# A hybrid decoder layer with expert retrieval on one core: gathers spread into the last expert group, one low half in four on GpSimd in the down stage, and one root chain with two output queues at the end

## The chip, the cores and the metric

The kernel runs on one core of one Trainium2 chip. The metric is the device time of one execution in microseconds (us), the median over the runs shown. A core has five instruction streams that matter here: TensorE (PE, matrix products), VectorE (DVE), ScalarE (ACT), GpSimd (POOL) and the sync engine (SP), which only issues transfers (DMAs). Each works through its own queue in order, and semaphores tie the queues together. PE writes to a small accumulator memory (PSUM); everything else lives in the on-chip buffer (SBUF) or in the device's main memory (HBM).

## The reference: what is computed

One decoder layer on 512 tokens of width 2048, in fp32. A first half mixes the tokens (projection, a gated MLP over the sequence, a matrix-memory recurrence, an output projection). The second half, where the change is, is a retrieval layer over 16384 experts: each token scores two sets of 128 keys per head, keeps 8 x 16 experts, and computes

```python
u_sel = peer_u.astype(xc.dtype)[eidx]
v_sel = peer_v.astype(xc.dtype)[eidx]
act = jax.nn.gelu(jnp.einsum("td,thkd->thk", xc, u_sel))
return jnp.einsum("thk,thkd->td", gate * act, v_sel)
```

That is followed by the residual sum and a last RMS norm: `x / sqrt(mean(x*x) + eps) * final_g`.

## The kernel before

**Two ways to the same sum.** For the last 352 tokens (`TD`) the kernel computes every expert, with dense products, and multiplies by a dense matrix of gates `Wd` that is zero where an expert is not chosen. For the first 160 tokens (128 and `G2` = 32 more) it gathers only the chosen rows of `peer_u` and `peer_v` with indirect DMAs, 128 rows (1 MB) in each, and DVE works on them. There are 2 x 128 + 2 x 32 = 320 gathers. Both ways run at the same time: PE does the dense one, and the gathers are spread over it.

**The dense way** has two stages. In the up stage (tile `pu`), for each of 128 groups of experts, the weights `in_u` are multiplied with the tokens. In the down stage (tile `pv`), 16 groups of experts (`g`) times 4 column chunks (`ch`) times 4 pieces (`pc`) of `in_v` are multiplied with `C`, the gated activations, which `product(g)` prepares one group ahead (`At` from `Ad`, `Wt` from `Wd`, lines 741 to 750 and 82). A piece is 128 x 1024 weights and 24 matmuls. To keep fp32 accuracy on a faster matmul type each operand is split in a high half (a rounded copy, ACT, line 109, tile `whi`) and a low half (the difference, line 110, tile `wlo`), and `mm3` issues three matmuls: line 118 and 119 need the high half of the weight, line 120 its low half.

**The path of a piece.** SP issues a 1 MB transfer `raw<-in_v` (line 102) that holds two pieces. There are two `raw` buffers, so SP waits until both low halves of the transfer two before are made. When it has landed, ACT makes two high halves, DVE two low halves, and PE uses them. `queue` holds `LA` = 3 pieces of lookahead. At the end of each chunk DVE adds four PSUM banks into `acc` (tile `top`, line 896: the evictions; one operand in PSUM, one in SBUF).

**The gathers.** `gather_step` is called after each piece and hands out gathers by a budget: the number left over the slots left, weighted with a share. A gather (line 572, on POOL) may not start before PE has finished the piece four calls earlier (`pace`), and needs one of three buffers `g`. DVE then reduces it: for `peer_u` a multiply and sum (line 608; the tokens lie in PSUM as `hps` in the up stage, in SBUF as `h` later), for `peer_v` a multiply and add into `acc0` or `acc1` (line 623, both inputs in SBUF).

**POOL's low halves.** In the up stage all low halves are put off (`defer["on"]`, list `pending`), and each `peer_u` gather's reduction hands one to POOL, with a dependency on a one-element DVE memset, the mark (tile `flag`, line 604). In the down stage before the change DVE makes all of them.

**Order.** The program is written in this order, but a scheduler with its own timeline then places the instructions of each engine. What stands in a queue is therefore read from the built program's order, as shown below.

**The end.** `settle` adds each finished chunk of 512 columns to the residual `xf` (three tiles of tokens, 96, 128 and 128 rows), with squares for the norm. For the last chunk it computes the root per tile and writes two halves per tile, six transfers, all on SP (line 875).

The lines of the budget and of the down loop before the change:

```python
gathers = {"left": 2 * P + 2 * G2, "slots": NP - 2 + NPC + nv - 24 - 28, "owed": 0.0}
...
def gather_step(last, share=1.0):
    pace.append(last.ins)
    gathers["owed"] += share * gathers["left"] / max(gathers["slots"], 1)
    gathers["slots"] -= share
...
for pc in range(GE // 2):
    hi, lo = take()
    if n + LA < nv:
        queue.append(next(weights))
```

## Time and profile before

| what | value |
|---|---|
| median of 3 runs | 2972.83 us (2971.12 to 2982.24) |
| the profiled execution: its time, its span | 2967.64 us, 2965.9 us |
| granted TensorE clock over the span | 0.991 |
| PE busy over the span | 2892.1 us (98%) |
| DVE, ACT, POOL busy | 2163.5, 1132.8, 794.1 us |
| HBM traffic | 798 MB, 269 GB/s over the span |

The up stage runs from about 820 to 1926 us of the span, the down stage from 1926 to about 2948 us. An engine's busy time is the union of its instructions' spans; PE's matmuls overlap, so PE can be busy without being at its peak. A row of a group gives line, engine, operation, tiles written and read, shapes and count; behind the bar total and mean duration, then the idle time in front and what ended it. "SPq" and the like are issuing instructions.

### The profile page before, as it was taken

To read this page: it belongs to the slowest core of one execution; us is meant where nothing else is said; L and a number is where in the kernel's file an instruction comes from. 1 tells how busy PE (TensorE), PEld (TensorE's weight loads), DVE (VectorE), ACT (ScalarE), POOL (GpSimd) and SP (SyncE) were. 2 spreads that over 40 slices of the span, in tenths; PEclk is the share of its full clock that TensorE was granted. 3 is DMA by queue.
4 is the path that set the end of the run, shared out by engine and by line. 5 is a ranking of instruction groups with operands and counts; after the bars stand their busy time and mean duration, and the time that the engine had idled before them with its cause. 6 is when DMAs were issued, how large, how long until landed. Compare 5 with 4: busy or idle time off the path is not lost.

```text
span 2965.9 us, 41624 instructions
## 1 busy us (share of the span) xinstructions
PE 2892.1 (98%) x16709; PEld 2725.1 (92%) x16709; DVE 2163.5 (73%) x3026; ACT 1132.8 (38%) x1635; POOL 794.1 (27%) x494
## 2 busy tenths in 40 slices
PE   9999999999999999999999999999999999999997
PEld 7888888887799999999999999999999999999997
DVE  5534333324696989979888887679988998889955
ACT  5322244323242333333676675323222323232333
POOL 0000000000046666565554211121232322223300
PEclk9999999999999999999999999999999999999999
DMA  6223222325379898888888888889999999999852
GB/s 241 86 86 121 86 92 93 102 97 178 114 272 349 337 344 335 308 336 299 334 341 344 336 346 335 321 322 367 376 358 344 365 364 344 375 341 368 338 199 105
DMA packets 147091, 800.78 MB, mean 270 GB/s; under 512 B 15168, under 2 KB 37744, under 8 KB 68656
## 3 DMA queue, kind: packets, MB, share of 16 engines
q1 hardware_dynamic: 87616, 401.68, 36.8%
q0 software_dynamic: 50064, 373.36, 33.3%
q10 hardware_dynamic: 9216, 23.07, 2.0%
q8 instruction: 131, 2.15, 0.3%
q14 instruction: 64, 0.52, 0.0%
HBM read 741.39 MB, written 56.62 MB: 269 GB/s over the span
## 4 chain that ended last, share of the span: by engine, by line
PE 80%; DVE 10%; DMA 6%; issue 2%; ACT 1%; SPq 0%; POOL 0%; ACTq 0%; DVEq 0%; POOLq 0%
PE pu L120 9%; PE pu L118 9%; PE pu L119 9%; PE pv L120 8%; PE pv L118 8%; PE pv L119 8%; PE pn L118 4%; PE pn L119 4%; PE pn L120 4%; DVE wlo L110 3%; PE pwb L725 3%; PE po L118 2%; PE po L120 2%; PE po L119 2%; DMA raw<-in_v 2%
## 5 line engine op out<-in xcount | busy, mean ns | idle before, releaser
L109 ACT ACTIVATE whi<-raw 128x1024 fp32r<-128x1024 f32 x512 | 526.9, 1055 | 850.6 <-DMA raw<-in_v 391.6
L120 PE MATMUL pu<-Th,wlo 128*128 128x352 f32 x2048 | 666.3, 325 | 17.5 <-DVE wlo L110 13.3
L118 PE MATMUL pu<-Th,whi 128*128 128x352 f32 x2048 | 673.7, 329 | 3.0 <-ACT whi L109 3.0
L118 PE MATMUL pv<-C,whi 128*128 128x352 f32 x2048 | 661.6, 324 | 6.7 <-ACT ast L795 3.9
L119 PE MATMUL pu<-Tl,whi 128*128 128x352 f32 x2048 | 664.4, 324 | 0.0
L119 PE MATMUL pv<-C,whi 128*128 128x352 f32 x2048 | 660.9, 323 | 0.0
L120 PE MATMUL pv<-C,wlo 128*128 128x352 f32 x2048 | 597.2, 325 | 16.1 <-DVE wlo L110 16.1
L110 DVE TENSOR_TENSOR wlo<-raw,whi 128x1024 fp32r<-128x1024 f32 x384 | 480.8, 1269 | 101.8 <-ACT whi L109 101.7
L572 POOL DMA_INDIRECT g<-in_peer_v,eidx x160 | 258.4, 1615 | 732.4 <-PE pv L120 276.6
L82 DVE TENSOR_TENSOR wlo<-raw,whi 128x1024 fp32r<-128x1024 f32 x130 | 159.2, 1225 | 350.4 <-ACT whi L81 350.1
L120 PEld LDWEIGHTS pu<-Th,wlo 128*128 128x128 f32 x2048 | 388.0, 189 | 19.9 <-DVE wlo L110 15.4
L120 PEld LDWEIGHTS pv<-C,wlo 128*128 128x128 f32 x2048 | 376.0, 189 | 22.3 <-DVE wlo L110 21.4
L118 PEld LDWEIGHTS pv<-C,whi 128*128 128x128 f32 x2048 | 386.7, 189 | 8.8 <-ACT ast L795 4.2
L623 DVE SCALAR_TENSOR_TENSOR acc<-g,gate,acc 128x2048 f32<-128x2048 f32 x160 | 375.8, 2348 | 23.5 <-DMA g<-in_peer_v,eidx 22.8
L118 PEld LDWEIGHTS pu<-Th,whi 128*128 128x128 f32 x2048 | 388.2, 190 | 4.5 <-ACT whi L109 4.0
L119 PEld LDWEIGHTS pu<-Tl,whi 128*128 128x128 f32 x2048 | 388.2, 190 | 0.4
L119 PEld LDWEIGHTS pv<-C,whi 128*128 128x128 f32 x2048 | 386.4, 189 | 0.8 <-issue 0.8
L110 POOL TENSOR_TENSOR wlo<-raw,whi 128x1024 fp32r<-128x1024 f32 x128 | 318.8, 2497 | 102.1 <-ACT whi L109 91.3
L608 DVE CUSTOM_DVE_ANT_0 g<-hps,g 128x2048 f32<-128x2048 f32 x128 | 291.6, 2283 | 44.5 <-DMA g<-in_peer_u,eidx 32.9
L572 POOL DMA_INDIRECT g<-in_peer_u,eidx x160 | 195.1, 1220 | 446.4 <-PE pv L120 99.8
L81 ACT ACTIVATE whi<-raw 128x1024 fp32r<-128x1024 f32 x130 | 137.6, 1058 | 443.6 <-PE pn L120 243.1
L119 PE MATMUL pn<-wlo,Th 128*128 128x512 f32 x512 | 205.1, 401 | 0.0
(275 smaller groups left out, 3510.4 us busy)
## 6 DMA issues: line engine op xcount, KB each, us to landing
raw<-in_u SPq DMA_DIRECT2D x128, 1024.0 KB
raw<-in_v SPq DMA_DIRECT2D x128, 1024.0 KB
raw<-in_w_in SPq DMA_DIRECT2D x80, 512.0 KB
Ad<-ast ACTq DMA_DIRECT2D x64, 352.0 KB
Wd<-wst POOLq DMA_DIRECT2D x11, 2048.0 KB
At<-Ad SPq DMA_DIRECT2D x32, 704.0 KB
raw<-in_w_out SPq DMA_DIRECT2D x32, 512.0 KB
Wt<-Wd SPq DMA_DIRECT2D x32, 512.0 KB
```

What stands on the lines that cost most here:

```text
L81: nc.scalar.activation(hi, src, AF.Copy)
L82: nc.vector.tensor_tensor(lo, src, hi.bitcast(F32), op=ALU.subtract)
L109: nc.scalar.activation(hi, part, AF.Copy)
L110: low = [lambda eng, lo=lo, part=part, hi=hi: eng.tensor_tensor(lo, part, hi.bitcast(F32), op=ALU.subtract)]
L118: nc.tensor.matmul(o, sh, mh, start=start, stop=False)
L119: nc.tensor.matmul(o, sh, ml, start=False, stop=False)
L120: return nc.tensor.matmul(o, sl, mh, start=False, stop=stop)
L572: i = nc.gpsimd.indirect_dma_start(out=g, out_offset=None, in_=table, in_offset=bass.IndirectOffsetOnAxis(ap=ix[:, q:q + 1], axis=0))
L608: nc.vector.tensor_tensor_reduce(out=g, in0=late["h"] if n == 0 and "h" in late else h[n], in1=g, op0=ALU.mult, op1=ALU.add, scale=1.0, sc ...
L623: nc.vector.scalar_tensor_tensor(acc[n], g, gt[:, q:q + 1], acc[n], op0=ALU.mult, op1=ALU.add)
L725: nc.tensor.matmul(pw[:, i * P:(i + 1) * P], o2[:, i, :], o1[:, i, :], start=True, stop=True)
```

## The change

The diff:

```diff
@@
                 mybir.DependencyClass.Sync, mybir.DependencyReason.DATA), reason="pace")
         return g
 
+    def beside():
+        while pending and not pending[0]:
+            pending.pop(0)
+        if pending:
+            mark = nc.vector.memset(flag, 0.0)
+            i = pending.pop(0).pop()(nc.gpsimd)
+            tc.add_manual_dep(i.ins, mark.ins.name, mybir.DependencyInfo(
+                mybir.DependencyClass.Sync, mybir.DependencyReason.DATA), reason="beside")
+
     acc2 = []
     late = {}
     DEPTH = 2
@@
                     h[1] = late["pool"].tile([P, D], F32, tag="h21", name="h21")
                     nc.sync.dma_start(h[1], h2d[1])
                 if n == 0 and "h" in late:
-                    while pending and not pending[0]:
-                        pending.pop(0)
-                    if pending:
-                        mark = nc.vector.memset(flag, 0.0)
-                        i = pending.pop(0).pop()(nc.gpsimd)
-                        tc.add_manual_dep(i.ins, mark.ins.name, mybir.DependencyInfo(
-                            mybir.DependencyClass.Sync, mybir.DependencyReason.DATA), reason="beside")
+                    beside()
                 nc.vector.tensor_tensor_reduce(out=g, in0=late["h"] if n == 0 and "h" in late else h[n], in1=g, op0=ALU.mult, op1=ALU.add, scale=1.0,
                                                scalar=0.0, accum_out=act[:, q:q + 1])
                 return
@@
     NPC = 2 * NE
     nv = 2 * NE
     exps = experts()
-    gathers = {"left": 2 * P + 2 * G2, "slots": NP - 2 + NPC + nv - 24 - 28, "owed": 0.0}
+    TURN = 0.6
+    gathers = {"left": 2 * P + 2 * G2, "slots": NP - 2 + NPC - 30 + 30 * TURN + 12 * TURN + nv - 12 - 14, "owed": 0.0}
 
     def gather_step(last, share=1.0):
         pace.append(last.ins)
@@
             if e % 2 == 1:
                 o = e % GE - 1
                 nc.scalar.dma_start(Ad[e // GE][:, o:o + 2, :], ast)
-        gather_step(last, 1.0 if begun is None else 0.45)
+        gather_step(last, 1.0 if begun is None else TURN)
         if not started:
             if not advance(first, 1):
                 started = n + 1
@@
         toks.append((at, min(P - at % P, T - at)))
         at += toks[-1][1]
     sq3 = vp.tile([P, 3, 4], F32, name="sq3")
+    nc.vector.memset(sq3, 1.0)
     ss3 = vp.tile([P, 4], F32, name="ss3")
     r3 = vp.tile([P, 4], F32, name="r3")
 
@@
             nc.scalar.activation(vp.tile([P, 512], F32, name="sj")[0:rows, 0:w.stop - w.start], o, AF.Square,
                                  accum_out=sq3[0:rows, j, ch:ch + 1])
             nc.vector.tensor_tensor(o, o, fg[0:rows, d], op=ALU.mult)
-            if not done:
-                continue
-            nc.vector.tensor_reduce(ss3[0:rows, j:j + 1], sq3[0:rows, j, :], axis=AX.X, op=ALU.add)
-            rstd(r3[0:rows, j:j + 1], ss3[0:rows, j:j + 1], D)
+        if not done:
+            return
+        nc.vector.tensor_reduce(ss3[:, 0:3], sq3, axis=AX.X, op=ALU.add)
+        rstd(r3[:, 0:3], ss3[:, 0:3], D)
+        for j, (t0, rows) in enumerate(toks):
             for hf in range(2):
-                s = slice(hf * 1024, (hf + 1) * 1024)
-                o = xf[j][0:rows, s]
+                o = xf[j][0:rows, hf * 1024:(hf + 1) * 1024]
                 if hf:
                     nc.scalar.activation(o, o, AF.Copy, scale=r3[0:rows, j:j + 1])
                 else:
                     nc.vector.tensor_scalar(o, o, r3[0:rows, j:j + 1], None, op0=ALU.mult)
-                nc.sync.dma_start(out[t0:t0 + rows, s], o)
+                (nc.sync, nc.gpsimd)[hf].dma_start(out[t0:t0 + rows, hf * 1024:(hf + 1) * 1024], o)
+
+    pick = vp.tile([P, G2], F32, name="pick")
+    nc.vector.tensor_reduce(pick, ident.rearrange("p (s t) -> p t s", t=G2), axis=AX.X, op=ALU.add)
+
+    def last_rows():
+        y = acc2[0]
+        for ch in range(4):
+            d = slice(ch * 512, (ch + 1) * 512)
+            ph = bank(("mm", "sm")[ch % 2], f"ph{ch}")
+            nc.tensor.matmul(ph[0:G2, :], pick, y[:, d], start=True, stop=True)
+            nc.scalar.activation(y[0:G2, d], ph[0:G2, :], AF.Copy)
+        finish(G2, y, hg.tile([P, D], F32, tag="g", name="junk", bufs=3), P)
 
     n = 0
     for g in range(NG):
@@
             for pc in range(GE // 2):
                 hi, lo = take()
                 if n + LA < nv:
+                    defer["on"] = pc == GE // 2 - 1
                     queue.append(next(weights))
+                    defer["on"] = False
                 for db in range(4):
                     last = part(pc, db, hi, lo)
                 n += 1
-                gather_step(last, 0.45 if n <= 12 else 1.0)
+                gather_step(last, TURN if n <= 12 else 1.0)
                 m = 4 * ch + pc
                 if m >= 10 or m % 2 == 0:
                     advance(nxt, 1)
+            beside()
             for db in range(4):
                 close(db)
             if g == NG - 1:
+                if ch == 1:
+                    assert gathers["left"] == 0, gathers
+                    advance(exps, 1)
+                    last_rows()
                 settle(ch, range(4), False)
         if g == NG - 2:
-            assert gathers["left"] == 0
-            advance(exps, 1)
-            y = acc2[0]
-            pick = vp.tile([P, G2], F32, name="pick")
-            nc.vector.tensor_reduce(pick, ident.rearrange("p (s t) -> p t s", t=G2), axis=AX.X, op=ALU.add)
-            for ch in range(4):
-                d = slice(ch * 512, (ch + 1) * 512)
-                ph = bank(("mm", "sm")[ch % 2], f"ph{ch}")
-                nc.tensor.matmul(ph[0:G2, :], pick, y[:, d], start=True, stop=True)
-                nc.scalar.activation(y[0:G2, d], ph[0:G2, :], AF.Copy)
-            junk = hg.tile([P, D], F32, tag="g", name="junk", bufs=3)
-            finish(G2, y, junk, P)
-            xf += [hg.tile([P, D], F32, tag="g", name=f"xf{j}", bufs=3) for j in range(3)]
+            xf += [At[0].rearrange("p j t -> p (j t)")[:, 0:D], Wt[0].rearrange("p b j t -> p (b j t)")[:, 0:D],
+                   hg.tile([P, D], F32, tag="h20", name="xf2")]
             for j, (t0, rows) in enumerate(toks):
                 nc.sync.dma_start(xf[j][0:rows, :], x2d[t0 // P, t0 % P:t0 % P + rows, :])
 
```

So the gathers' budget has 487.2 slots instead of 460, and the gathers end inside the last group of experts instead of before it; the residual tiles `xf` now lie in buffers that are free earlier, since the `g` buffers are still in use. Of the four pieces fetched during a chunk the last one's low half is put off and handed to POOL where the chunk's evictions are written, with the same kind of mark as in the up stage. At the end one chain of small operations serves all three tiles, and the second half of each tile's output goes out over POOL's queue.

Three places in the built programs' order. The first is DVE's queue before the up stage, while the query weights are split (line 82); `flag` is the mark that POOL's low halves wait for. The last marks of before, and what follows them:

```order
L604 MEMSET flag_4784 1x1 x26
L82 TENSOR_TENSOR wlo_4980<-raw_4978,whi_4979 128x1024
L604 MEMSET flag_4784 1x1 x27
L82 TENSOR_TENSOR wlo_5010<-raw_5008,whi_5009 128x1024
L604 MEMSET flag_4784 1x1 x9
L82 TENSOR_TENSOR wlo_5048<-raw_5046,whi_5047 128x1024
```

The same place after:

```order
L583 MEMSET flag_4784 1x1 x26
L82 TENSOR_TENSOR wlo_4980<-raw_4978,whi_4979 128x1024
L583 MEMSET flag_4784 1x1 x27
L82 TENSOR_TENSOR wlo_5010<-raw_5008,whi_5009 128x1024
L583 MEMSET flag_4784 1x1 x26
L82 TENSOR_TENSOR wlo_5048<-raw_5046,whi_5047 128x1024
L583 MEMSET flag_4784 1x1 x27
L82 TENSOR_TENSOR wlo_5094<-raw_5092,whi_5093 128x1024
L583 MEMSET flag_4784 1x1
L492 MAX val_5076<-sc_5080 128x8 x2
L583 MEMSET flag_4784 1x1
L493 MAX_INDEX ind_5077<-val_5076,sc_5080 128x8 x2
```

All 128 marks before, and all 191 after, are placed there, far ahead of the stages whose low halves wait for them; the 63 new ones have not moved to the evictions.

The second place is POOL's queue in the down stage, at the fourth group of experts. Numbers tell the buffers apart; `wlo_18244` is the low half of a piece, `raw` and `whi` its transfer and its high half. Before:

```order
L572 DMA g_18441<-in_peer_v,eidx_4618 128x2048
L572 DMA g_18475<-in_peer_v,eidx_4618 128x2048
L572 DMA g_18537<-in_peer_v,eidx_4618 128x2048
L572 DMA g_18578<-in_peer_v,eidx_4618 128x2048
L572 DMA g_18642<-in_peer_v,eidx_4618 128x2048
L572 DMA g_18675<-in_peer_v,eidx_4618 128x2048
L572 DMA g_18745<-in_peer_v,eidx_4618 128x2048
L572 DMA g_18776<-in_peer_v,eidx_4618 128x2048
```

After:

```order
L572 DMA g_18373<-in_peer_v,eidx_4618 128x2048
L110 TENSOR_TENSOR wlo_18244<-raw_18241,whi_18243 128x1024
L572 DMA g_18444<-in_peer_v,eidx_4618 128x2048
L572 DMA g_18478<-in_peer_v,eidx_4618 128x2048
L572 DMA g_18539<-in_peer_v,eidx_4618 128x2048
L572 DMA g_18582<-in_peer_v,eidx_4618 128x2048
L110 TENSOR_TENSOR wlo_18380<-raw_18377,whi_18379 128x1024
L572 DMA g_18646<-in_peer_v,eidx_4618 128x2048
L572 DMA g_18678<-in_peer_v,eidx_4618 128x2048
L110 TENSOR_TENSOR wlo_18513<-raw_18510,whi_18512 128x1024
L572 DMA g_18750<-in_peer_v,eidx_4618 128x2048
L572 DMA g_18781<-in_peer_v,eidx_4618 128x2048
```

A low half now stands after every two to four gathers, in one queue with them: it starts when the gathers ahead of it are issued and its high half is made, and the gathers behind it wait for it. In DVE's queue 63 rows of line 110 are gone (384 before, 321 after).

The third place is the end of SP's queue. Before:

```order
L938 DMA xf_24109<-x2d 96x2048
L938 DMA xf_24110<-x2d 128x2048
L938 DMA xf_24111<-x2d 128x2048
L846 DMA out<-acc_22275 32x2048
L102 DMA raw<-in_v 128x2048 x4
L875 DMA out<-xf_24109 96x1024 x2
L875 DMA out<-xf_24110 128x1024 x2
L875 DMA out<-xf_24111 128x1024 x2
L999 UNCONDITIONAL_BRANCH
```

After, the end of SP's queue:

```order
L951 DMA Wt_15254<-x2d 128x2048
L102 DMA raw<-in_v 128x2048 x5
L951 DMA At_15253<-x2d 96x2048
L102 DMA raw<-in_v 128x2048 x13
L851 DMA out<-acc_22766 32x2048
L880 DMA out<-At_15253 96x1024
L880 DMA out<-Wt_15254 128x1024
L880 DMA out<-xf_24133 128x1024
L1012 UNCONDITIONAL_BRANCH
```

After, the end of POOL's:

```order
L110 TENSOR_TENSOR wlo<-raw,whi 128x1024
L572 DMA g<-in_peer_v,eidx_4783 128x2048 x3
L110 TENSOR_TENSOR wlo<-raw,whi 128x1024
L572 DMA g<-in_peer_v,eidx_4783 128x2048
L110 TENSOR_TENSOR wlo<-raw,whi 128x1024 x3
L880 DMA out<-At_15253 96x1024
L880 DMA out<-Wt_15254 128x1024
L880 DMA out<-xf_24133 128x1024
L1012 UNCONDITIONAL_BRANCH
```

The six transfers of the output are three and three now; the two loads of `xf` that stood behind the bulk of `raw<-in_v` are 13 and 18 transfers ahead of its end (the third, `xf_24133`, is further ahead still).

## The prediction

> **What bounds the kernel now.** I read the page first, then the granted clock, then the down stage cut into stretches, then the waits of PE, SP and POOL in it, and last the groups of DVE. The page and the stretches (columns: length, then busy time and count of PE, weight loads, DVE, ACT, POOL, then granted clock, DMA share, GB/s):
>
> ```profile
> span 2965.9 us, 41624 instructions
> 1926.00:2080.00 154.00, 153.65 (x951) 153.66 (x952) 126.43 (x109) 44.82 (x43) 33.05 (x24) 0.99 0.91 346
> 2080.00:2780.00 700.00, 681.10 (x4199) 674.87 (x4198) 628.76 (x557) 210.13 (x203) 209.23 (x121) 0.99 0.94 358
> 2780.00:2878.00 98.00, 98.00 (x615) 97.63 (x614) 69.04 (x67) 30.17 (x30) 15.55 (x8) 1.00 0.66 246
> 2878.00:2948.00 70.00, 70.00 (x432) 66.31 (x431) 37.58 (x55) 25.57 (x39) 0.00 (x0) 1.00 0.36 121
> 2948.00:2966.00 18.00, 1.08 (x10) 0.84 (x8) 7.59 (x31) 5.93 (x12) 0.00 (x0) 0.68 0.45 161
> ```
>
> PE is the bound nearly everywhere. It loses time in one place of the down stage, from 2080 to 2780 us: 18.9 us of 700. There DVE is busy for 629 of 700 us (89.8%) and the DMA engines 94%. In the stretch before, at 82% and 91%, PE loses 0.35 us; behind 2780 us, where the gathers thin out and end, it loses nothing. So the place for a gain is 18.9 us of idle PE and what the clock loses after such pauses:
>
> ```profile
> 2200.00:2300.00 100.00, 95.87 (x587) 95.00 (x586) 87.94 (x72) 28.84 (x28) 29.90 (x17) 0.98 0.93 356
> 2400.00:2500.00 100.00, 95.43 (x573) 94.26 (x574) 87.59 (x83) 32.06 (x32) 25.61 (x17) 0.97 0.93 348
> ```
>
> 0.02 and 0.03 of 100 us are 5 us of clock. What PE waits for there, and SP and POOL:
>
> ```profile
> PE pv L120 <- DVE wlo L110: 16.1, 17, 2.6
> ...
> SPq L102 <- DVE wlo L110: 402.9, 80, 10.2
> ...
> SPq L745 <- DVE At L750: 74.8, 10, 12.6
> ...
> POOL g L572 <- PE pv L120: 267.7, 66, 8.4
> ```
>
> PE waits for low halves, 17 times; SP waits to issue the next transfer of weights until the low halves of an older one are made; so a late DVE makes the transfer late, and this the next high and low half. POOL mostly waits for PE's pace, which is harmless. What DVE does in these 700 us:
>
> ```profile
> L110 DVE TENSOR_TENSOR wlo<-raw,whi 128x1024 fp32r<-128x1024 f32 x176 | 209.9, 1219 | 6.9 <-ACT whi L109 6.9
> L623 DVE SCALAR_TENSOR_TENSOR acc<-g,gate,acc 128x2048 f32<-128x2048 f32 x89 | 209.1, 2349 | 9.1 <-DMA g<-in_peer_v,eidx 8.7
> L896 DVE TENSOR_TENSOR top<-pv,top 128x352 f32<-128x352 f32 x175 | 88.0, 520 | 50.5 <-PE pv L120 48.0
> L608 DVE CUSTOM_DVE_ANT_0 g<-h,g 128x2048 f32<-128x2048 f32 x32 | 72.9, 2287 | 0.4 <-DMA g<-in_peer_u,eidx 0.3
> L82 DVE TENSOR_TENSOR C<-At,C 128x1408 fp32r<-128x1408 f32 x22 | 35.7, 1621 | 3.7 <-ACT C L81 3.4
> L750 DVE TENSOR_TENSOR At<-At,Wt 128x1408 f32<-128x1408 f32 x22 | 35.7, 1621 | 0.0
> ```
>
> All but the evictions (L896) have both tensors in SBUF: 209.9 + 209.1 + 72.9 + 35.7 + 35.7 = 563 us, 80% of the time.
>
> **The change, part by part.** The sum is made against the profiled execution, 2967.6 us, and its differences are put on the median, 2972.8, which is 5.2 us (0.17%) above it.
>
> *Gathers spread further.* 320 gathers over 487.2 instead of 460 slots: 5.6% thinner. In the 700 us there are 121 (89 + 32 rows above), so 7 fewer: 7 x 2.35 = 16 us less DVE, and 7 MB less of 358 GB/s x 700 us = 251 MB, 2.8%. Against this stand the loads of `xf`, 2.9 MB in all, of which the first two now fall in or just behind this stretch (1 to 2 MB), and one more wait of the kind SP on L750, 7.5 us each (74.8 by 10), which lies before a transfer and may or may not reach PE. Net some 5 MB, 2%, and the DMA share falls to about 0.92, near the stretch without loss. The load goes to 2780 to 2870 us, where DVE has 29 of 98 us free and the DMA share is 0.66: some 7 x 2.35 = 16 us more DVE, 87% then.
>
> *One low half in four to POOL.* DVE loses 44 of 176: 44 x 1.22 = 54 us. But the order shows the marks in DVE's queue before the up stage, 2000 us ahead, so nothing ties a POOL low half to the evictions; it starts when its turn comes in POOL's queue. What it then does to DVE the up stage shows, where 128 of them run. First the group, then two meetings:
>
> ```profile
> L110 POOL TENSOR_TENSOR wlo<-raw,whi 128x1024 fp32r<-128x1024 f32 x128 | 318.8, 2497 | 102.1 <-ACT whi L109 91.3 <-PE pwb L725 4.1 <-DVE inf L515 1.3
> L110 DVE TENSOR_TENSOR wlo<-raw,whi 128x1024 fp32r<-128x1024 f32 x64 | 96.8, 1514 | 26.3 <-ACT whi L109 26.3
> ...
> 1388.08 2.40 POOL L110 TENSOR_TENSOR wlo<-raw,whi 128x1024 fp32r<-128x1024 f32 x1
> 1387.69 3.88 DVE L110 TENSOR_TENSOR wlo<-raw,whi 128x1024 fp32r<-128x1024 f32 x1
> ...
> 941.10 2.41 POOL L110 TENSOR_TENSOR wlo<-raw,whi 128x1024 fp32r<-128x1024 f32 x1
> 942.21 2.29 DVE L608 CUSTOM_DVE_ANT_0 g<-hps,g 128x2048 f32<-128x2048 f32 x1 [2.54 <-DMA g<-in_peer_u,eidx]
> ```
>
> A DVE subtraction with both inputs in SBUF takes 3.88 instead of 1.22 us beside POOL's 2.40: it stands still while POOL works. A DVE operation with one input in PSUM (`hps`) keeps its 2.29. Over the up stage the 64 DVE low halves take 1.51 instead of 1.22 us. By this row alone POOL's 128 cost DVE 64 x 0.30 = 19 us, 0.15 each: the lower bound. The upper is a whole POOL operation, 2.41. In the down stage 80% of DVE's time are such operations, so a POOL operation at a random moment costs 0.80 x 2.41 = 1.9 us; some will fall beside evictions, and I take 1.6, nearer to the upper end for that share. Then DVE's account is 54 saved, 44 x 1.6 = 70 paid: +16 us, and the thinner gathers give 16 back. DVE's share stays at 90%. Both ends for the range: from 54 + 16 - 7 = 63 us less (81%, as in the stretch without loss) to 54 + 16 - 106 = 36 us more (95%).
>
> The Trainium skill (SBUF — State Buffer, section "Who interferes with whom") says that a VectorE instruction with two SBUF inputs and a GpSimd one that reads SBUF exclude each other for the whole instruction, and that the one that issues first keeps the other waiting. The 3.88 above agrees, and by that rule alone each low half outside the evictions costs the full 2.41; what that gives is the second rival.
>
> *POOL's queue.* A low half waits at its head for its high half, with gathers behind it. In the up stage PE waited for a POOL low half once in 128:
>
> ```profile
> PE pu L120 <- DVE wlo L110: 13.3, 6, 4.2
> PE pu L120 <- POOL wlo L110: 4.1, 1, 4.1
> ...
> L572 POOL DMA_INDIRECT g<-in_peer_v,eidx x89 | 158.8, 1784 | 353.0 <-PE pv L120 167.9 <-DVE acc L623 97.0 <-DVE top L896 30.4
> ```
>
> 63 new ones at that rate are 2 us. The upper bound: where a gather ahead is released late, it takes 1.78 us, then DVE's running operation up to 2.35, then 2.41, 6.5 together against less than two pieces (a piece is 700 us / 175 = 4.0); a fifth of the 63 late by 1 us each are 13 us. I take 3.
>
> *Result for the down stage.* With DVE unchanged and the DMA share halfway back to where nothing is lost, I take a third off: 18.9 / 3 + 5 / 3 = 8 us gained. The rate that is left, 12.6 us in 700, goes on for 90 us: 1.6 lost. POOL late: 3 lost. Net -3.4.
>
> *The up stage.* POOL and DVE do the same work with gathers 5.6% thinner at first and denser at the turn (0.6 for 0.45). Its waits are 17.4 us in the two rows above, and a new order may move them either way by 5; I take -1.
>
> *`last_rows`.* Moved, not new, into a part where PE is 100% and DVE 54% busy (37.58 of 70). Zero, as long as the last gather is reduced before PE comes to it; two chunks are left to hide it.
>
> *The end.* SP's six issues, and the two engines that feed them:
>
> ```profile
> 2954.61 5.55 SPq L875 DMA_DIRECT2D out<-xf  x6
> ...
> 2953.82 3.23 ACT L872 ACTIVATE xf<-xf,r 96x1024 f32<-96x1024 f32 x3 [0.56 <-DVE r L78]
> ...
> 2954.76 1.41 DVE L874 TENSOR_SCALAR xf<-xf,r 128x1024 f32<-128x1024 f32 x2
> ```
>
> The last half tile is ready at 2957.05 (ACT), the last issue ends at 2960.16. With two queues the issue is no longer 3.1 us behind, but 2.9 MB at the 346 to 358 GB/s of the stretches above take 8 us, and the end is at 2965.9, 11.3 us after the first issue. So at most 3 us, at least -1 (a slower start on POOL's queue); I take 1.4 gained. The single root chain makes the first tile wait for the third, and spares small operations: zero. The Trainium skill (DMA: Bandwidth & Descriptors, section "Issuing engines are not separate DMA queues") has transfers of all issuing engines run on the same 16 engines; by that too the second queue can spare issue time alone.
>
> Sum: -3.4 - 1 - 1.4 = -5.8, rounded to -6: **2967 us**, 0.2% under the median and within the 0.5% (15 us) that a measurement of this kernel can tell from no change.
>
> **The rivals.** *Faster:* POOL's low halves fall beside evictions or idle time after all ((88 + 71) / 700 = 23% of DVE's time are evictions or idle), DVE drops to 81%, the DMA share to 0.92, and the down stage runs like 1926 to 2080 us. Then 18.9 + 5 go, the up stage gives some 2, the end 1.4: -27, 2946 us. For it: PE waits for nothing but low halves. Against it: the marks tie nothing, and 80% of DVE's time is of the kind that stands still. From half of this on, -15, it counts as faster. *Slower:* each POOL low half holds DVE for its full length: DVE 95%. From 82% to 90% PE's loss went from 0.2% to 2.7%, 0.32% per point; 5 points more are 1.6% of 800 us at the least, 13 us, and twice that if it goes on steepening, plus up to 13 for late POOL halves: +15 to +39, say 2995 us. It decides from a cost per low half of about 2 us on. This is also where the Trainium skill's rule of exclusion (SBUF — State Buffer, "Who interferes with whom") leads if it is taken strictly. *The marks do nothing:* the order shows it, so it is part of the forecast and has no chance of its own.
>
> **How the numbers follow.** Forecast, anywhere from 2958 to 2988, 0.49; faster rival 0.30; slower rival 0.21. The range 2942 to 2995 takes in the faster rival and half of the slower one. The likeliest case's own range is 2958 to 2980.
>
> **What would show it.** PE's idle time in 2080 to 2780 falls to about 12 us and something is left up to 2870; 63 POOL rows of line 110 in the down stage at 2.4 to 3 us; DVE's add (L623) and low halves longer by 70 us together; the DMA share there 0.92; waits of PE for POOL's low half a few us; the span's last transfers closer together. I am wrong if DVE's operations keep their length (then faster), or if PE waits for POOL, or for DVE behind it, by more than 30 us (then slower).

## The result, and the profile after

| kernel | median of the runs | ratio to before, 95% interval |
|---|---|---|
| before | 2971.97 us (2966.85 to 2982.24, 4 runs) | |
| after | 3010.39 us (3004.44 to 3013.16, 4 runs) | 1.0123 [1.0098, 1.0148] |

The change makes the kernel 38 us slower. The forecast was 2967 us and its range ended at 2995.

The profiled execution after took 3012.83 us, 45.2 more than the one shown of before. In the trace, first to last `pv` matmul (the down stage) grew from 1021.1 to 1053.4 us, +32.3. The up stage (first `pu` to first `pv`) grew from 1108.3 to 1115.8, +7.5, and the time from the last eviction's end to the end of the span from 17.6 to 19.1, +1.5. The other 3.9 lie ahead of the up stage. The down stage after, cut in the same stretches as before and moved by 12 us (length, then busy time and count of PE, weight loads, DVE, ACT, POOL, then granted clock, DMA share, GB/s):

```profile
span 3011.1 us, 41826 instructions
1938.00:2092.00 154.00, 150.73 (x914) 150.15 (x914) 122.83 (x97) 43.73 (x42) 62.83 (x31) 0.98 0.87 335
2092.00:2792.00 700.00, 676.82 (x4142) 670.09 (x4141) 622.27 (x497) 207.61 (x199) 312.90 (x155) 0.99 0.91 345
2792.00:2890.00 98.00, 88.05 (x524) 86.59 (x523) 84.98 (x61) 27.21 (x26) 39.78 (x22) 0.97 0.86 320
2890.00:2990.00 100.00, 99.63 (x604) 95.54 (x605) 67.86 (x74) 33.01 (x46) 23.77 (x11) 0.98 0.47 172
```

DVE's share in the 700 us is 622.27 / 700 = 88.9% (before 89.8%) and the DMA share 0.91: both as forecast. PE's idle time there is 23.2 us instead of 18.9. But the two stretches beside it, which lost 0.35 us together before, now lose 3.3 and 10.0. Over the four rows PE is idle for 36.8 us, against 19.3 before; that is 17.5 of the 32.3. The rest is PE being busy longer with the same 6144 matmuls. The granted clock is 0.97 to 0.98 in three of the four rows (before 0.99 to 1.00); its mean over the stage went from 0.993 to 0.984, which is some 10 us. What PE waited for in the 700 us, and DVE's and GpSimd's groups:

```profile
PE pv L120 <- POOL wlo L110: 11.5, 8, 2.8
PE pv L120 <- DVE wlo L110: 8.7, 12, 1.7
...
L626 DVE SCALAR_TENSOR_TENSOR acc<-g,gate,acc 128x2048 f32<-128x2048 f32 x81 | 205.6, 2538 | 3.5 <-DMA g<-in_peer_v,eidx 2.9
L110 DVE TENSOR_TENSOR wlo<-raw,whi 128x1024 fp32r<-128x1024 f32 x129 | 189.4, 1479 | 26.4 <-ACT whi L109 26.2
L913 DVE TENSOR_TENSOR top<-pv,top 128x352 f32<-128x352 f32 x172 | 85.2, 516 | 39.6 <-PE pv L120 38.9
L611 DVE CUSTOM_DVE_ANT_0 g<-h,g 128x2048 f32<-128x2048 f32 x32 | 80.8, 2538 | 0.0
L82 DVE TENSOR_TENSOR C<-At,C 128x1408 fp32r<-128x1408 f32 x22 | 46.5, 2112 | 7.6 <-ACT C L81 7.6
L754 DVE TENSOR_TENSOR At<-At,Wt 128x1408 f32<-128x1408 f32 x20 | 35.1, 1756 | 0.0
...
L110 POOL TENSOR_TENSOR wlo<-raw,whi 128x1024 fp32r<-128x1024 f32 x43 | 129.5, 3011 | 57.6 <-ACT whi L109 53.7 <-DVE top L913 3.2
```

Here `acc` is the add of a gathered row, `g<-h` its product, and `C` and `At` belong to `product(g)`. Each mean is compared with that of before. Adds: 81 x 0.189 us; low halves: 129 x 0.260; `g<-h`: 32 x 0.251; `C`: 22 x 0.491; `At`: 20 x 0.135. That is 15.3 + 33.5 + 8.0 + 10.8 + 2.7 = 70 us, 1.63 us for each of the 43 low halves on GpSimd (1.6 was forecast). The evictions, one input in PSUM, keep their 0.52. GpSimd's own operation takes 3.01 us, where the one of the up stage took 2.50. So DVE's share, its price per low half and the DMA share came out as forecast; PE's idle time (12 us was forecast) and the time did not.

### The profile page after: what moved, and what is told of

It is laid out like the page before. It is cut to its first block, busy times and chain, and to the rows that moved or that the text cites. A ratio compares the mean times of both kernels' runs of the same rounds, so it can differ in the third digit from the quotient of the medians.

```text
span 3011.1 us, 41826 instructions
## 1 busy us (share of the span) xinstructions
PE 2913.4 (97%) x16709; PEld 2740.3 (91%) x16709; DVE 2206.6 (73%) x3013; ACT 1135.2 (38%) x1633; POOL 963.7 (32%) x560
## 4 chain that ended last, share of the span: by engine, by line
PE 71%; DVE 16%; DMA 7%; issue 4%; ACT 1%; POOL 1%; SPq 0%; DVEq 0%; POOLq 0%; ACTq 0%
PE pu L120 8%; PE pu L119 8%; PE pu L118 8%; PE pv L120 7%; PE pv L118 6%; PE pv L119 6%; DVE wlo L110 4%; PE pn L118 4%; PE pn L120 4%; PE pn L119 4%; DVE g L611 3%; DMA raw<-in_v 2%; DVE acc L626 2%; PE pwb L729 2%; PE po L120 2%
## 5 line engine op out<-in xcount | busy, mean ns | idle before, releaser
L120 PE MATMUL pu<-Th,wlo 128*128 128x352 f32 x2048 | 665.1, 325 | 15.8 <-DVE wlo L110 15.8
L120 PE MATMUL pv<-C,wlo 128*128 128x352 f32 x2048 | 630.0, 328 | 32.4 <-DVE wlo L110 19.1
L110 POOL TENSOR_TENSOR wlo<-raw,whi 128x1024 fp32r<-128x1024 f32 x191 | 508.2, 2662 | 267.4 <-ACT whi L109 256.6
L110 DVE TENSOR_TENSOR wlo<-raw,whi 128x1024 fp32r<-128x1024 f32 x321 | 462.0, 1449 | 106.0 <-ACT whi L109 105.6
L572 POOL DMA_INDIRECT g<-in_peer_v,eidx x160 | 242.4, 1515 | 594.1 <-PE pv L120 221.1
L626 DVE SCALAR_TENSOR_TENSOR acc<-g,gate,acc 128x2048 f32<-128x2048 f32 x160 | 400.6, 2504 | 36.8 <-DMA g<-in_peer_v,eidx 35.8
L120 PEld LDWEIGHTS pv<-C,wlo 128*128 128x128 f32 x2048 | 384.8, 191 | 40.9 <-DVE wlo L110 24.2
L82 DVE TENSOR_TENSOR wlo<-raw,whi 128x1024 fp32r<-128x1024 f32 x130 | 159.0, 1223 | 346.8 <-ACT whi L81 338.3
L120 PEld LDWEIGHTS pu<-Th,wlo 128*128 128x128 f32 x2048 | 387.3, 189 | 19.1 <-DVE wlo L110 19.0
## 6 DMA issues: line engine op xcount, KB each, us to landing
raw<-in_u SPq DMA_DIRECT2D x128, 1024.0 KB, 7.0
raw<-in_v SPq DMA_DIRECT2D x128, 1024.0 KB, 7.3
```

Source lines behind the costliest of these rows:

```text
L82: nc.vector.tensor_tensor(lo, src, hi.bitcast(F32), op=ALU.subtract)
L110: low = [lambda eng, lo=lo, part=part, hi=hi: eng.tensor_tensor(lo, part, hi.bitcast(F32), op=ALU.subtract)]
L120: return nc.tensor.matmul(o, sl, mh, start=False, stop=stop)
L572: i = nc.gpsimd.indirect_dma_start(out=g, out_offset=None, in_=table, in_offset=bass.IndirectOffsetOnAxis(ap=ix[:, q:q + 1], axis=0))
L626: nc.vector.scalar_tensor_tensor(acc[n], g, gt[:, q:q + 1], acc[n], op0=ALU.mult, op1=ALU.add)
```

## The experiments

Every experiment is told by two numbers: the median of its runs with its ratio to the kernel before (with the 95% interval), and the down stage of its profiled execution. Lines of edits or of a view that are left out are marked by three dots. Four kernels with the down stage's code of before had 1017.5 to 1022.8 us there in their profiles, so differences under about 5 us in a single profile say nothing. The up stage's profiles scatter more (1102 to 1126 us, the code of before alike), so the medians carry less than the down stage does.

### Each part of the change alone

**Everything but the low halves.** Edit against after:

```diff
-                    defer["on"] = pc == GE // 2 - 1
                     queue.append(next(weights))
-                    defer["on"] = False
...
-            beside()
             for db in range(4):
```

> The changed kernel with all low halves of the down stage on DVE again; the gathers' budget, the later last rows and the new end stay. Theory L (the loss in the down stage is GpSimd's low halves): the down stage goes back from 1053 to about 1022 us, the 11 us of the up stage stay: about 2981 to 2984 us. Theory G (the loss is the gathers, which now fall into stretches that lost nothing before): the down stage stays above 1040 us, about 3000 us or more.

Theory L holds. Measured: 2978.27 us, 1.0017 [1.0001, 1.0033]; down stage 1018.1 us. Without them the loss of the down stage is gone.

**The low halves alone**, in the kernel before. The expectation calls the piece the fourth, since it is the fourth that is fetched during a chunk; three pieces of lookahead make it the third of the next chunk, and it is called the third below.

```diff
+                    defer["on"] = pc == GE // 2 - 1
                     queue.append(next(weights))
+                    defer["on"] = False
...
+            beside()
             for db in range(4):
```

> The kernel before with one change: the fourth low half of each chunk of the down stage goes to GpSimd. Theory L: the down stage takes 1045 to 1053 us instead of 1022, 2995 to 3003 us in all, and DVE's low halves there take 1.4 to 1.5 us instead of 1.22. Theory G: the kernel before within 0.3%, 2965 to 2980 us. In both the up stage is as before, 1926 us.

Measured: 2998.79 us, 1.0092 [1.0078, 1.0106]; down stage 1051.7, up stage 1108.9 us. Theory L holds: +30.6 us of the 32.3. Its 700 us and waits:

```profile
2080.00:2780.00 700.00, 667.28 (x4083) 657.04 (x4082) 639.77 (x500) 207.70 (x200) 333.05 (x161) 0.99 0.91 349
...
PE pv L120 <- DVE wlo L110: 15.1, 14, 2.5
PE pv L120 <- POOL wlo L110: 12.9, 11, 2.7
...
L110 POOL TENSOR_TENSOR wlo<-raw,whi 128x1024 fp32r<-128x1024 f32 x43 | 132.1, 3072 | 51.8 <-ACT whi L109 37.1 <-PE pv L119 11.9 <-DVE top L899 2.4
```

**The gathers alone** (the budget, the share 0.6, `last_rows` and `xf` as in the change; the rest as before), by its core:

```diff
-    gathers = {"left": 2 * P + 2 * G2, "slots": NP - 2 + NPC + nv - 24 - 28, "owed": 0.0}
+    TURN = 0.6
+    gathers = {"left": 2 * P + 2 * G2, "slots": NP - 2 + NPC - 30 + 30 * TURN + 12 * TURN + nv - 12 - 14, "owed": 0.0}
```

> The kernel before with the gathers' part alone: budget, share at the turn 0.6, last rows and the xf loads moved. Theory L: the up stage ends 11 us later, the down stage takes 1015 to 1025 us: 2975 to 2985 us. Theory G: 2995 to 3005 us, with PE losing 15 us or more in the 120 us behind the 700 us stretch and in the 150 us ahead of it.

Measured: 2973.16 us, 1.0003 [0.999, 1.0016]; down stage 1015.2 us; from 2780 to 2900 us PE loses 0.5 us:

```profile
2780.00:2900.00 120.00, 119.53 (x747) 119.24 (x746) 103.58 (x87) 36.05 (x35) 28.47 (x20) 1.00 0.90 335
```

Theory G falls: the 10 us that PE lost there after came with GpSimd's low halves, not with the gathers.

**The end alone** (root chain and two queues):

```diff
+        nc.vector.tensor_reduce(ss3[:, 0:3], sq3, axis=AX.X, op=ALU.add)
+        rstd(r3[:, 0:3], ss3[:, 0:3], D)
...
+                (nc.sync, nc.gpsimd)[hf].dma_start(out[t0:t0 + rows, hf * 1024:(hf + 1) * 1024], o)
```

> The kernel before with the new end alone: one root chain, two queues. By the trace after, the time from the last eviction to the end is 19.6 instead of 18.1 us: +1.5, 2973 to 2975 us where the kernel before has 2972. By the prediction it is -1.4, 2970 to 2971 us. Both are near what the medians can tell; the profile's time from the last eviction on decides.

Measured: 2977.95 us, 1.0014 [0.9999, 1.0029]; 19.2 us from the last eviction, against 17.0 to 17.6 in the kernels with the old end. The end costs 1.6 to 2.2 us. The median is 6.7 us longer, but the up stage of this profile, with the code of before, is one of the long ones (1125.7 us), so the rest says nothing of the end.

### Why one low half costs 0.5 us of time

Theory X: DVE stands still while GpSimd reads SBUF. Theory Q: the loss comes from the wait in GpSimd's queue. Four kernels leave out the low half that the change moves (PE's third matmul reads the high half instead), and three of them put something else in its place in GpSimd's queue. The ground step:

```diff
+            if "on" in skip and skip["on"]:
+                hi = hi.rearrange("p (j d) -> p j d", j=2)
+                nc.scalar.activation(hi, part, AF.Copy)
+                yield hi, hi, None
+                continue
...
+                    skip["on"] = pc == GE // 2 - 1
                     queue.append(next(weights))
+                    skip["on"] = False
```

> The kernel before with the fourth low half of each chunk of the down stage left out (the third matmul reads the high half instead): DVE saves what the change takes from it, and GpSimd gets nothing. All theories: DVE's share from 2080 to 2780 us falls from 90% to about 82%, PE loses a few us there instead of 19, the down stage takes about 1000 instead of 1021 us, 2950 us in all. If it stays above 1015 us, DVE's load was not what PE waited for, and the change had nothing to win.

Measured: 2971.86 us, 1.0002 [0.9982, 1.0022]; down stage 1020.2 us. The 1000 us were missed and the last sentence holds: with the operations gone altogether, nothing is won.

```profile
2080.00:2780.00 700.00, 681.38 (x4207) 675.74 (x4207) 581.82 (x515) 211.80 (x204) 179.05 (x121) 1.00 0.94 359
...
PE pv L126 <- DVE wlo L116: 12.7, 14, 2.2
```

DVE is busy for 83% instead of 90%, and PE still loses 18.6 us, 12.7 of it waiting for DVE's low halves (L116 and L126 are L110 and L120 here). An engine with 118 us of free time was late all the same.

**A memset in the queue**, tied to the high half (`skip["act"]` is ACT's copy):

```diff
...
+                i = nc.gpsimd.memset(S, 0.0)
+                tc.add_manual_dep(i.ins, skip["act"].ins.name, mybir.DependencyInfo(
+                    mybir.DependencyClass.Sync, mybir.DependencyReason.DATA), reason="beside")
```

> As the kernel with the low halves left out, and in GpSimd's queue a memset of 128 x 1024 stands in the place of each of its low halves, which waits for the same high half; nobody waits for it. It takes GpSimd's queue as the low half does, but reads nothing. Theory Q (the loss comes from GpSimd's queue, gathers standing behind a low half that waits): the down stage goes above 1030 us. Theory X (the loss comes from DVE's standing still while GpSimd reads SBUF): within 6 us of the kernel with the low halves left out, and DVE's operations as long as before (1.22, 2.35 us).

Measured: 2974.72 us, 1.0011 [0.9988, 1.0035]; down stage 1024.0 us. **About as long as the low half** (2.45 us), with two and a half memsets:

```diff
...
+                for j in range(3):
+                    i = nc.gpsimd.memset(S if j < 2 else S[:, 0:512], 0.0)
...
```

> As the kernel with the memsets, but two and a half of them in a row, 0.96 + 0.96 + 0.5 us, as long as GpSimd's subtraction (2.3 to 2.4 us) without reading anything. If the 14 us between the memset and the subtraction (1024.0 and 1038.3 us of down stage) come from DVE's standing still, this one stays at 1022 to 1028 us; if they come from the longer time in GpSimd's queue, it takes 1034 to 1042 us.

Measured: 2975.56 us, 1.0009 [0.999, 1.0028]; down stage 1025.1 us. **A subtraction that reads SBUF**, with nobody waiting for it:

```diff
...
+                nc.gpsimd.tensor_tensor(S.rearrange("p (j d) -> p j d", j=2), skip["hi"].bitcast(F32), skip["hi"].bitcast(F32), op=ALU.subtract)
```

> The same with a subtraction of the high half from itself into an unused tile in GpSimd's queue: it reads two inputs in SBUF as the low half does, but neither PE nor the weights' transfers wait for its result. Theory X: DVE's low halves and adds longer by 1.5 to 1.8 us per GpSimd operation (about 110 us in the down stage), the down stage 25 us or more above the kernel with the memsets, 1030 to 1045 us. Theory Q: as with the memsets, within 6 us. What is then missing to the 1052 us of the real low halves is what PE and the transfers pay for waiting for GpSimd.

Measured: 2989.24 us, 1.0065 [1.0039, 1.0091]; down stage 1038.3 us. The memsets' groups (GpSimd), their stretch, and that of the subtraction:

```profile
L931 POOL MEMSET S<- 128x1024 f32 x88 | 84.6, 961 | 46.7 <-ACT whi L109 44.1
L931 POOL MEMSET S<- 128x512 f32 x44 | 23.3, 529 | 2.2
...
2080.00:2780.00 700.00, 679.61 (x4187) 674.79 (x4187) 580.40 (x511) 212.28 (x205) 279.19 (x253) 0.99 0.94 358
```

```profile
2080.00:2780.00 700.00, 670.55 (x4109) 665.52 (x4108) 628.35 (x502) 208.59 (x200) 298.07 (x162) 0.98 0.92 352
...
L117 DVE TENSOR_TENSOR wlo<-raw,whi 128x1024 fp32r<-128x1024 f32 x128 | 193.7, 1528 | 24.5 <-ACT whi L116 24.4
L930 POOL TENSOR_TENSOR S<-whi 128x1024 f32<-128x1024 f32 x43 | 99.0, 2303 | 61.0 <-ACT whi L109 55.4 <-DVE wlo L117 5.0
```

Memsets of 961 + 961 + 529 ns, longer than the 2303 ns of the subtraction, leave DVE's 580 us as they were without them (582); the subtraction makes them 628. ACT never waits for GpSimd there, so it is not the high half's buffer being read longer that costs the time. The Trainium skill (SBUF — State Buffer, "Who interferes with whom") says that a VectorE instruction with two SBUF inputs contends with a GpSimd instruction that reads SBUF and not with one that only writes it; this pair agrees with that.

So theory X holds, and of theory Q at most the 5 us of the occupied queue are left. The staircase, in us of down stage: left out 1020.2; occupied queue 1025.1 (+5, at the edge of the scatter); reading SBUF 1038.3 (+13); the real low half 1051.7 (+13). The last step has two parts that no run separates. PE waits for GpSimd (12.9 us in 11 cases), and so does SP before it issues a transfer (11 times). But the low half, with two different inputs, also takes GpSimd 3.07 us instead of 2.30 and holds DVE for 1.9 us instead of 1.5, by the sum made above for the kernel after. The subtraction also shows why a busy share cannot forecast this: DVE is busy for 628.35 us, before the change for 628.76. PE loses 29.5 us in the one and 18.9 in the other.

**Tied to the evictions.** The marks tied nothing; here the low half waits for PE's last matmul of the chunk's second bank.

```diff
-            mark = nc.vector.memset(flag, 0.0)
+            mark = by or nc.vector.memset(flag, 0.0)
...
-            beside()
+            beside(second)
```

> The kernel before with GpSimd's low halves in the down stage, each now tied to PE's last matmul of the chunk's second bank, so that it starts where DVE's evictions stand (the marks tied nothing). Theory X: DVE stands still about 1.0 instead of 1.7 us for each (the evictions cover some of it), the down stage takes about 1035 us, better than the 1052 us without the tie and still worse than 1021. Theory Q: GpSimd's low halves are later than without the tie, PE waits longer for them, 1055 us or more.

Measured: 2999.85 us, 1.0102 [1.0069, 1.0135]; down stage 1051.5 us. Neither theory's number: the tie changes nothing. The trace shows why: the low halves start 4.4 us behind the matmul that they are tied to (median), and 4.1 us behind the same matmul without the tie. They were waiting for something else, and evictions run beside 14% of their time, against 13% without the tie.

### Which low half is late

For each low half of the down stage I took the time from its end to PE's first use of it, and counted those with less than 0.3 us, by the place of the piece in its chunk (a few could not be matched):

| kernel | first | second | third | fourth |
|---|---|---|---|---|
| before | 18 of 62 | 0 of 62 | 4 of 63 | 0 of 63 |
| after | 16 of 61 | 3 of 60 | 9 of 60 (GpSimd) | 0 of 61 |

The change moves the third. The late one is the first, and DVE's and PE's rows of before show why:

```profile
2201.88 1.62 DVE L750 TENSOR_TENSOR At<-At,Wt 128x1408 f32<-128x1408 f32 x1
2203.42 2.34 DVE L623 SCALAR_TENSOR_TENSOR acc<-g,gate,acc 128x2048 f32<-128x2048 f32 x1
2205.68 1.38 DVE L896 TENSOR_TENSOR top<-pv,top 128x352 f32<-128x352 f32 x3
2206.97 1.22 DVE L110 TENSOR_TENSOR wlo<-raw,whi 128x1024 fp32r<-128x1024 f32 x1
2208.11 0.52 DVE L896 TENSOR_TENSOR top<-pv,top 128x352 f32<-128x352 f32 x1
...
2207.70 0.32 PE L119 MATMUL pv<-C,whi 128*128 128x352 f32 x1
2208.24 0.43 PE L120 MATMUL pv<-C,wlo 128*128 128x352 f32 x1 [0.22 <-DVE wlo L110]
```

The high half was ready at 2201.1 us. Its low half (2206.97) stands in DVE's queue behind a product, an add and three evictions, and an eviction cannot start before PE ends its bank, which is when PE asks for the low half. The other late ones look alike: 16 of the 18 started the moment that DVE was done with the operation before, and 17 stood directly behind an eviction. That is theory F; theory D is that the transfers set the pace (DMA share 0.94).

**The first low half left out**, in place of the third:

```diff
-                    skip["on"] = pc == GE // 2 - 1
+                    skip["on"] = pc == 1
```

> As the kernel with one low half in four left out, but the first of each chunk in place of the third. In the trace before, 18 of 62 first low halves end less than 0.3 us ahead of PE's use of them, and 4 of 63 third ones (the ones that the change moves). Theory F (PE waits for the first low half, which stands in DVE's queue behind the evictions of the chunk before): PE loses under 8 us from 2080 to 2780 instead of 19, the down stage takes 1000 to 1008 us. Theory D (the transfers set the pace, whatever DVE does): 1018 to 1022 us, as with the third left out.

Measured: 2958.78 us, 0.9950 [0.9933, 0.9967]; down stage 1005.1 us. Theory F:

```profile
2080.00:2780.00 700.00, 692.82 (x4307) 691.18 (x4307) 595.84 (x526) 215.30 (x208) 181.07 (x124) 1.00 0.96 368
...
PE pv L124 <- ACT whi L109: 6.8, 3, 3.0
```

PE loses 7.2 us instead of 18.6, and no longer waits for a low half. DVE is busier than with the third left out (596 us against 582), and the transfers run faster (368 against 359 GB/s), so they had room.

**The first on GpSimd**, handed over at once:

```diff
-                    defer["on"] = pc == GE // 2 - 1
+                    defer["on"] = pc == 1
...
+                if pc == 1:
+                    beside()
```

> The kernel before with the first low half of each chunk on GpSimd instead of the third, handed over as soon as it is written in the program. Theory F with the price of DVE's standing still: 10 to 15 us better than the 1052 us of the third, since a part of the late ones goes, and still slower than before: 1035 to 1042 us, 2985 to 2990 us in all. Theory D: 1050 us, as with the third.

Measured: 2983.46 us, 1.0038 [1.0013, 1.0062]; down stage 1034.7 us. Moving the right low half is 17 us better than moving the third, and still 13.6 us worse than moving none: 24 of 62 third low halves, back on DVE, are now late, and in the 700 us PE waits 11.1 us for GpSimd's low halves and 10.2 for DVE's.

**The order alone**, nothing on GpSimd: the evictions behind the next chunk's first low half in DVE's queue.

```diff
+                if n + LA < nv:
+                    tc.add_manual_dep(i.ins, lows[-LA].ins.name, mybir.DependencyInfo(
+                        mybir.DependencyClass.NoSync, mybir.DependencyReason.DATA), reason="ahead")
```

> The kernel before, nothing on GpSimd; in DVE's queue the evictions of a chunk are ordered behind the first low half of the next chunk (an order, no wait). Theory F: PE loses under 10 us from 2080 to 2780, the down stage takes 1003 to 1012 us, about 2958 us in all, faster than both kernels. Theory D: 1018 to 1024 us, no change.

Measured: 2965.97 us, 0.9976 [0.9957, 0.9995]; down stage 1013.9 us, PE's loss in the 700 us 12.7. It is 0.24% faster than before, and its down stage and PE's loss fall short of theory F's numbers. Late first low halves fell from 18 to 4 of 62; what PE now waits for most are two high halves:

```profile
2080.00:2780.00 700.00, 687.31 (x4253) 685.49 (x4252) 629.30 (x561) 212.79 (x206) 208.81 (x122) 0.99 0.95 363
...
PE pv L119 <- ACT whi L110: 8.0, 2, 6.8
PE pv L121 <- DVE wlo L111: 4.7, 3, 2.1
```

**The same with the gathers' part**, both edits in one kernel:

> The same order in the kernel with the gathers' part of the change (gathers going on into the last group), with the old end and nothing more on GpSimd. The gathers' part alone took 1015 us for the down stage, 6 less than before, and some 8 us more for the up stage. Theory F: the down stage takes 998 to 1008 us, 2955 to 2965 us in all. Theory D: 1012 to 1018 us, 2970 to 2976 us.

Measured: 2980.48 us, 1.0020 [1.0001, 1.0039]; down stage 1015.6 us. Theory F's number missed: the two gains do not add. The gathers' part alone already brings the late first low halves from 18 to 8, and the order brings either kernel to 4, so both remove the same ones. That the median is longer than with either part alone stays open.

### The gathers' share, and the end

**The gathers' part with the old share 0.45 at the turn** (the slots follow from it):

```diff
-    TURN = 0.6
+    TURN = 0.45
```

> The kernel with the gathers' part alone, with the old share of 0.45 at the turn (slots adapted). In the profiles of the four kernels with the gathers' part PE loses 5 to 6 us between 1600 and 1760 us of the up stage, where those without it lose nothing, and waits 4 to 7 us there for ACT's part of the gate matrix (pwb). If the share at the turn does it, this loss is gone here and the time is 2964 to 2970 us; if the thinner gathers and the other order that they bring do it, it stays: 2970 to 2976 us. Down stage 1014 to 1018 us in both.

Measured: 2954.78 us, 0.9935 [0.9915, 0.9955], the fastest kernel here; down stage 1009.5 us. PE between 1600 and 1760 us, with the share 0.6 (gathers alone) and then 0.45:

```profile
1600.00:1760.00 160.00, 154.25 (x998) 152.74 (x997) 122.78 (x114) 104.92 (x203) 53.91 (x33) 0.97 0.79 301
...
PE pwb L729 <- ACT o L728: 3.3, 4, 1.5
```

```profile
1600.00:1760.00 160.00, 157.87 (x1063) 157.06 (x1062) 129.09 (x123) 112.94 (x223) 56.60 (x34) 1.00 0.86 324
...
PE pwb L729 <- ACT o L728: 1.1, 2, 0.7
```

The loss falls from 5.8 to 2.1 us, so the share at the turn is most of it. The medians differ by 18 us, far more, and the time lies below both forecasts. In the two profiles the up stage is 13 us shorter (1111.8 against 1124.9) and the down stage 6; the clock in the stretch shown, 0.97 against 1.00, is some 5 us of it. Where the rest lies I could not show, since single up stages scatter by more than that. **With the order of the evictions added:**

> The gathers' part alone with the share 0.45 at the turn, and the evictions ordered behind the next chunk's first low half. If the two gains add (down stage 1009.5 us by the thinner gathers, 1013.9 us by the order, 1021.1 without either): about 1003 us and 2948 us in all. If both remove the same late low halves: 1008 to 1012 us, 2953 to 2958 us, as without the order.

Measured: 2961.73 us (2955.16 to 2981.37), 0.9956 [0.9934, 0.9978]. The profiled execution, 2980.5 us, is one of its long ones (down stage 1024.8), so the stage tells nothing. The gains do not add; whether the order even harms here stays open.

**One root chain, all on SP**, and **two queues, a chain for each tile**, against the new and the old end:

```diff
-                (nc.sync, nc.gpsimd)[hf].dma_start(out[t0:t0 + rows, hf * 1024:(hf + 1) * 1024], o)
+                nc.sync.dma_start(out[t0:t0 + rows, hf * 1024:(hf + 1) * 1024], o)
...
-                nc.sync.dma_start(out[t0:t0 + rows, s], o)
+                (nc.sync, nc.gpsimd)[hf].dma_start(out[t0:t0 + rows, s], o)
```

> The kernel before with one root chain for the three tiles of tokens and all six output transfers on SP. From the last eviction to the end the kernel before takes 17.6 us (17.0 to 17.6 in all kernels with the old end), those with the new end 18.9 to 19.2. If the second queue costs the 1.6 us, this one takes 17.0 to 17.7; if the common root chain does, 18.7 to 19.3.

> The kernel before with a root chain for each tile of tokens and the output transfers in turn on SP and GpSimd's queue. If the second queue costs the 1.6 us: 18.7 to 19.3 us from the last eviction to the end; if the common root chain does: 16.5 to 17.6.

Measured, in one profile each: 18.0 us from the last eviction with the common chain, 18.8 with the two queues; 17.0 to 17.6 with neither. The queue costs 1.2 to 1.8 us, as expected if it is the cause; the chain's 0.4 to 1.0 us lie between its two forecasts and are as small as the scatter. SP's and GpSimd's issues of the second:

```profile
2952.00 1.91 SPq L875 DMA_DIRECT2D out<-xf  x3
...
2952.65 1.60 POOL L875 DMA_DIRECT2D out<-xf  x2 [137.25 <-ACT xf L872]
2954.73 0.54 POOL L875 DMA_DIRECT2D out<-xf  x1 [0.48 <-ACT xf L872]
```

By the packets' records SP's first packet moves 0.83 us behind its first issue (2952.83 us), GpSimd's 2.76 us behind its own (2955.41). The last byte is there at 2961.88, and the span ends 2.6 us later. So it does in all four kernels with GpSimd's queue at the end; in the fifteen with SP alone it takes 1.4 to 1.9 us.

## Why the prediction was wrong

- **What bounds the kernel.** PE's waits for low halves were read rightly, but as one group. By place in the chunk they were the first ones (18 of the 22 late ones), and the change takes the third. I read DVE's 90% as the cause; leaving 7 points of it away gained nothing, leaving away the right operation gained 16 us.
- **The failed step** is "With DVE unchanged and the DMA share halfway back to where nothing is lost, I take a third off: 18.9 / 3 + 5 / 3 = 8 us gained." The step took it that with DVE's busy share unchanged PE's waits would not grow: in the sum the low halves stand with nothing for DVE and 3 us for POOL's queue. DVE's share stayed and the DMA share fell, as said, and the low halves alone cost 30.6 us. What the runs show in place of that step: standing still for 1.6 us at a time adds to the lateness of whatever is queued behind it, while the 1.22 us saved came off operations that PE had waited for once, for 0.7 us. Put back on DVE in the changed kernel, the low halves leave PE 7.5 us of waits for first low halves and 2.3 for third ones; with the change they are 18.6 and 13.3.
- **The clock** was put at 5 us and a third of it taken off; over the stage it cost some 10 us more instead.
- **The cost of a GpSimd low half to DVE:** 1.6 us forecast, 1.63 measured, 1.9 with the low halves alone. The size was right, with some luck in the digits: it was worked out for an operation of 2.41 us, and the operation took 3.01. Its conversion into time was wrong.
- **POOL's queue:** 3 us taken, 13 the upper bound. PE's own waits for GpSimd are 11.5 us in 8 cases in the 700 us; the staircase's last step, 13 us, holds these and a longer hold on DVE. The rate of the up stage (one wait in 128) did not carry over.
- **The gathers:** they gained some 6 us in the down stage when alone (1015.2 against 1021.1; 2 to 8 against the four profiles of the old code), about the 8 us of the failed step, which came from them. In the up stage they lost 5 to 6 us between 1600 and 1760 us, where I had taken 1 gained. Going on to 2870 us cost nothing by itself, and `last_rows` stayed hidden (99.63 of 100 us busy).
- **The end:** 1.4 gained was forecast with a bound of 1 lost; 1.6 to 2.2 were lost. I weighed the issue time, and set 1 us for a slower start of GpSimd's queue (its first packet came 1.9 us later behind its issue than SP's) and nothing for its close (0.8 us or more).
- **The slower rival** had the sign and, at its upper end, the size (+15 to +39), but mostly by DVE at 95%, which did not occur. Its up to 13 us for late GpSimd low halves did.
- **The marks** tie nothing, as the order showed; the one tie that was tried did not help.

## What to carry to other kernels

Before work is taken off a busy engine, sort the waits for it by which instance is late: an engine at 83% was as late as one at 90%, because the late operation stood in its queue behind others that wait for the consumer itself. Ask what stands ahead of the late one, and move that. Work moved to an engine that blocks the first one while it runs is paid as lateness of what stands behind it, which a busy share does not show.

## What the runs showed of the hardware

GpSimd and DVE slow each other. GpSimd's subtraction of 128 x 1024 took 2.50 us on average in the up stage, 3.01 to 3.07 among DVE's two-input work in the down stage, and 2.30 where both of its inputs were the same tile. In the trace of before, the 22 of the up stage that met no DVE operation with all its tensors in SBUF took at most 2.42 us, and the others up to 3.89. A GpSimd memset of the same size took 0.96 us and cost DVE nothing. The two kinds of queue differ at both ends of a transfer: the first packet of the output moved 0.83 us (SP) and 2.76 us (GpSimd) behind the issue, and the program ended 1.4 to 1.9 us behind the last byte with SP alone, 2.6 us with GpSimd's queue.
